# Six weight loads moved ahead of a branch and onto GpSimd's DMA queue, in a mixture-of-experts decoder layer

## The chip, the core and the metric

The kernel runs on one core of a Trainium2 chip. A core has five engines that follow their own instruction streams: TensorE (PE in the profile; its weight loads are PEld), VectorE (DVE), ScalarE (ACT), GpSimd (POOL) and SyncE (SP). SP does no arithmetic here; it issues transfers from the chip's main memory. Transfers issued by any engine are carried out by the core's 16 DMA engines. The metric is the device time of one execution in microseconds (us); smaller is better.

## What is computed

One layer of a hybrid decoder for 256 tokens of width 1024, all in 32-bit floats: two token mixers and an output projection, then a mixture of experts (MoE), then a gated embedding and a norm. The change lies in the MoE. Each token is given the two best of 32 experts, and each expert is a small gated network (the reference, cut; `xt` are the normed tokens, `wr` the routing weights):

```python
def blk(args):                       # one block of rows of one expert e
    ...
    xb = xt[toks]
    hid = jax.nn.silu(xb @ w_gate[e]) * (xb @ w_up[e])      # 1024 -> 512
    return ((hid @ w_down[e]) * wr[:, None]).astype(xt.dtype)  # 512 -> 1024
...
y = jax.ops.segment_sum(yb.reshape(n_pad, d), row_tok, num_segments=T)
```

No row may be dropped: an expert takes as many tokens as are sent to it.

## The kernel before

The mixers come first, then the experts in order, 0 to 31, in eight groups of four (`QUAD`, `NQ`, the loop over `q`). Each expert has room for 32 tokens (`CAP`). For a group, `dispatch` (L739) gathers the tokens of its four experts with one-hot matmuls (tile `px`, L761) into `xe`. For each expert, `expert` (L785) multiplies by the gate and up weights (`pg`, L810, eight blocks `k` of the 1024 inputs), applies SiLU (`sg`, L814) and the product (`hid`, L816), transposes (`pht`, L818, copied to `hT`), and multiplies by the down weights (`pd`, L827) into `eo`. After four experts `combine` (L837; tile `ps`, L839) adds the group's rows back into the tokens `h`.

An expert's weights are 6 MB: two loads of gate and up weights (here gu1 for blocks 0 to 3 and gu2 for blocks 4 to 7, 2 MB each, L712) and one load of down weights (dn, 2 MB, L717). I write 16gu1 for the first load of expert 16, 16dn for its last. Each load takes one slot of a ring of ten slots of 2 MB (`NRING`, all tiles named `wt`), in program order. A slot is written again when the matmuls on its old contents are done, so a load takes the slot of the load ten places before it: 16gu1 takes that of 12dn, 18gu1 that of 14dn, 18dn that of 15gu2, and 19gu2 that of 16gu1.

All loads are issued by SP, in order. Each of SP's loads signals one of eight completion semaphores in turn (`DMAHW0` to `DMAHW7` in the rows below), and waits until the load before it on the same semaphore has landed. So SP never has more than eight loads under way.

A token beyond the 32 of an expert is handled by `overflow` (L845), which stands after group 3 (`LOOP_AT`). It counts the rows per expert, works out how many extra blocks there are (`n_it`, L875), and every engine reads that number (L876) and branches on it:

```python
n_rv = nc.values_load(n_it[0:1, 0:1], min_val=0, max_val=NITEM, ...)   # L876
with tc.If(n_rv > 0):                                                  # L878
    with tc.For_i(0, n_rv, 1):                                         # L879
```

With these inputs the loop body is not entered. A scheduler orders the instructions of each engine between such branches; in the kernel before it has put the two gate and up loads of expert 16 ahead of the branch on SP, and all later ones behind it. On the way past the branch SP executes an instruction that waits for all eight of its completion semaphores.

Of the kernel before, what the change touches and what calls it, by code (L numbers as in the profile page):

```python
# [29 lines left out]
QUAD = 4  # L30
# [7 lines left out]
LO_POOL = (11, 101)  # L38
NRING = 10
LOOP_AT = 3  # L40

MIX = ["aq", "ak", "av", "mq", "mk", "mv", "mo", "ga", "ga1", "gm", "gm1"]
IN_OFF = dict(aq=0, ak=512, av=1024, mq=1536, mk=2048, mv=2560, mo=3072, mi=3584, mf=3588,
# [4 lines left out]
def layer(ctx: ExitStack, tc: tile.TileContext, A, dbg=None):  # L48
    nc = tc.nc
# [9 lines left out]
    def slot(shape, dt=F32, name="wt"):  # L59

        return ring.tile(shape, dt, name=name, tag="ring")
# [20 lines left out]
    for nm, src in (  # L82
# [7 lines left out]
        n = src.shape[0]  # L90
# [57 lines left out]
    for c in range(2):  # L148
        t = slot([P, 2, 4, 512])
# [66 lines left out]
    def split(dst_hi, dst_lo, src, scale=None, lo_on=None, low=False):  # L216

        if scale is None:
            a = nc.scalar.activation(dst_hi, src, AF.Copy)  # L219
            b = (lo_on or nc.vector).tensor_tensor(dst_lo, src, dst_hi.bitcast(F32), op=OP.subtract)  # L220
        else:
            a = nc.scalar.activation(dst_hi, src, AF.Copy, scale=scale)
            b = nc.vector.scalar_tensor_tensor(dst_lo, src, scale, dst_hi.bitcast(F32),
                                               op0=OP.mult, op1=OP.subtract)
        return b if low else a
# [63 lines left out]
    for k in range(KD):  # L289
# [13 lines left out]
        wt = wts["mq"][:, k].rearrange("p (f n) -> p f n", f=4)  # L303
# [280 lines left out]
    for f in range(0, KD, 2):  # L584
        pA = psf.tile([P, 2, T], F32, name="po", tag="po", bufs=3)
        wt, c0 = wup[f // 4], (f % 4) * P
# [121 lines left out]

    wgu_v, wd_v = A["expert_gu"], A["expert_down"]

    def load_gu(t, e, k0, n):
        nc.sync.dma_start(out=t, in_=wgu_v[e][:, k0:k0 + n])  # L712
        return [t[:, k] for k in range(n)]

    def load_expert(e):
        def load_dn(t, j, n):
            nc.sync.dma_start(out=t, in_=wd_v[e][:, j:j + n])  # L717
            return [t[:, i] for i in range(n)]

        gu = load_gu(slot([P, 4, 2, 512]), e, 0, 4)  # L720
        if e == NRING // 3:

            for k in range(4, 6):
                gu += load_gu(mo.tile([P, 1, 2, 512], F32, name="ov", tag="ov"), e, k, 1)
            t = slot([P, 4, D])
            gu += load_gu(t[:, 0:2].rearrange("p k (a n) -> p k a n", a=2), e, 6, 2)
            dn = load_dn(t[:, 2:4], 0, 2) + load_dn(slot([P, 2, D]), 2, 2)
        else:
            gu += load_gu(slot([P, 4, 2, 512]), e, 4, 4)
            t = slot([P, 4, D])  # L730
            if e == NE - 1:
                dn = load_dn(t[:, 0:2], 0, 2) + load_dn(t[:, 2:4], 2, 2)
            else:
                dn = load_dn(t, 0, 4)
        return gu, dn
# [101 lines left out]
    def combine(dwT, eo, n, b, c):  # L837
        ps = psm.tile([P, 512], F32, name="ps", tag="ps", bufs=2)
        mm(ps, dwT[0:n, b], eo[0:n, c * 512:(c + 1) * 512], start=True, stop=True)  # L839
        cs = slice(c * 512, (c + 1) * 512)  # L840
        return nc.vector.tensor_tensor(h[:, b, cs], ps, h[:, b, cs], op=OP.add)
# [63 lines left out]
    def embed():  # L905
        wpp = slot([P, 2, D], name="wpp")
        nc.sync.dma_start(out=wpp, in_=A["w_ple_proj"])
        ES = slot([P, 4096], name="ES")
        pin = ES[:, 0:512].rearrange("p (b n) -> p b n", b=NB)
        pT = ES[:, 512:1024].rearrange("p (k t) -> p k t", k=2)  # L910
        pe = ES[:, 1024:3072].rearrange("p (b n) -> p b n", b=NB)
        gfin = ES[:, 3072:4096]
        nc.sync.dma_start(out=pin, in_=A["p"].rearrange("l o (b p) d -> p (l o b) d", p=P))
        pp = psm.tile([P, 2, T], F32, name="pp", tag="tp", bufs=2)
        for k in range(2):
            for b in range(NB):
                nc.tensor.transpose(pp[:, k, b * P:(b + 1) * P], pin[:, b, k * P:(k + 1) * P], ident)
        nc.scalar.activation(pT, pp, AF.Copy)
        for b in range(NB):
            for c in range(2):  # L920
                ps = psm.tile([P, 512], F32, name="ps", tag="ps", bufs=2)
                for k in range(2):
                    mm(ps, pT[:, k, b * P:(b + 1) * P], wpp[:, k, c * 512:(c + 1) * 512],  # L923
                       start=(k == 0), stop=(k == 1))
                nc.scalar.activation(pe[:, b, c * 512:(c + 1) * 512], ps, AF.Copy, scale=0.5)
        return pe, gfin


    def load_gate():
        out = []  # L930
        for q in range(2):
            wt = slot([P, 4, D])
            for k in range(0, 4, 2):
                nc.sync.dma_start(out=wt[:, k:k + 2], in_=A["w_ple_gate"][q][:, k:k + 2])
            out.append(wt)
        nc.sync.dma_start(out=gfin, in_=A["final_norm_g"].rearrange("(o d) -> o d", o=1).to_broadcast([P, D]))
        return out

    def split_gate(k):
# [2 lines left out]
        hi, lo = gw[k // 4]  # L942
        return split(hi[:, k % 4], lo[:, k % 4], wpl[k // 4][:, k % 4], lo_on=nc.gpsimd if k in (0, 1, 3, 5) else None)

    for q in range(NQ):
        dwT, xe, rest = dispatch(float(q * QUAD * ESTR) if q else None, code, P)
        eo = mo.tile([P, D], F32, name="eo", bufs=1)
        for i in range(QUAD):
            e = q * QUAD + i
            wt = load_expert(e)  # L950
            if e == NE - 1:
                wpl = load_gate()
            expert(wt, xe, i, eo, 32 * i, last=(e == NE - 1), rest=rest if i == 0 else None)
        if q < NQ - 1:
            for c in range(2):
                for b in range(NB):
                    combine(dwT, eo, P, b, c)
        if q == LOOP_AT:
            overflow()
        if q == NQ - 3:  # L960
            pe, gfin = embed()
# [135 lines left out]
```

## Time and profile before

| | |
|---|---|
| time, median of 3 runs (lowest to highest) | 706.93 us (704.91 to 707.18) |
| the profiled execution: its time / its span | 706.04 us / 704.3 us |
| busy share of the span, PE / DVE / ACT / POOL | 80% / 40% / 26% / 5% |
| moved by DMA | 241.98 MB, mean 344 GB/s |
| chain that ended last: DMA / PE | 48% / 44% |

The span is what the trace covers; the 1.7 us between it and the execution's time lie outside. The chain is the sequence of work that ended last, followed back from the end; its DMA share is time in which an engine at the end of the chain waited for a transfer. Busy shares are averages over stages with different limits: the first 220 us or so are the mixers, with PE busy and DMA in part; from there to about 660 us run the experts.

### The profile page before, as it was taken

The numbers are of one execution on the slowest core, as the hardware profiler recorded it, in microseconds if no ns is written. First come the engines' busy times: TensorE is split into PE (matmuls) and PEld (weight loads), VectorE is DVE, ScalarE is ACT, GpSimd is POOL, SyncE is SP. The second block draws the span as 40 slices with busy tenths as digits, with TensorE's granted clock in tenths as the row PEclk, the third lists the DMA queues.
The fourth block names the chain that finished last, engine by engine and source line by source line (L and its number), as shares of the span: only waits on it lengthen the run. The fifth ranks groups of instructions, "written<-read, shape, count | busy, mean of one in ns | idle before, by whom it ended". The sixth has DMA issues, their size and how long they took to land.

```text
span 704.3 us, 12210 instructions
## 1 busy us (share of the span) xinstructions
PE 560.9 (80%) x5161; PEld 382.3 (54%) x5161; DVE 280.7 (40%) x684; ACT 186.1 (26%) x423; POOL 38.2 (5%) x59
## 2 busy tenths in 40 slices
PE   7999999999999998685686564967746956765894
PEld 7898778899986554342334231733423433432384
DVE  4898667676665343141022024312211310311175
ACT  6675556465453211001000000010000210000163
POOL 3000000001300000000000000000000000000063
PEclk9999999999999999899669886898978997988998
DMA  7946533338777899999999997999999999999921
GB/s 268 429 205 248 228 122 120 120 120 333 305 327 299 333 428 428 428 424 429 423 428 426 430 426 316 429 423 430 426 426 424 425 427 427 429 428 424 419 99 60
DMA packets 22130, 241.98 MB, mean 344 GB/s; under 512 B 4708, under 2 KB 5304, under 8 KB 7096
## 3 DMA queue, kind: packets, MB, share of 16 engines
q1 hardware_dynamic: 22056, 241.16, 82.5%
q8 instruction: 42, 0.69, 0.4%
q14 instruction: 16, 0.13, 0.0%
q10 hardware_dynamic: 16, 0.00, 0.0%
HBM read 240.10 MB, written 1.05 MB: 342 GB/s over the span
## 4 chain that ended last, share of the span: by engine, by line
DMA 48%; PE 44%; DVE 4%; ACT 2%; issue 1%; POOL 1%; POOLq 0%; SPq 0%; DVEq 0%; ACTq 0%
DMA wt<-in_expert_gu 31%; DMA wt<-in_expert_down 17%; PE pg L810 5%; PE po L330 4%; PE po L331 4%; PE po L332 4%; PE ps L839 3%; PE po L347 2%; PE po L346 2%; PE po L348 2%; PE pd L827 2%; PE px L761 2%; PE ps L923 1%; PE pyy L470 1%; DMA wt<-in_w_mix 1%
## 5 line engine op out<-in xcount | busy, mean ns | idle before, releaser
L810 PE MATMUL pg<-wt,xe 128*32 128x256 f32 x2032 | 153.6, 438 | 69.8 <-DMA wt<-in_expert_gu 69.8
L810 PEld LDWEIGHTS pg<-wt,xe 128*32 128x32 f32 x2032 | 73.3, 122 | 136.8 <-issue 55.6
L827 PE MATMUL pd<-wt,hT 128*32 128x256 f32 x1024 | 73.6, 434 | 22.8 <-DMA wt<-in_expert_down 18.6
L833 DVE COPY eo<-pd 32x256 f32<-32x256 f32 x64 | 27.1, 423 | 114.5 <-ACT eo L835 114.4
L827 PEld LDWEIGHTS pd<-wt,hT 128*32 128x32 f32 x1024 | 37.9, 121 | 47.4 <-issue 32.9
L835 ACT ACTIVATE eo<-pd 32x256 f32<-32x256 f32 x64 | 23.9, 374 | 150.3 <-PE pd L827 132.0
L816 DVE TENSOR_TENSOR hid<-sg,pg 128x128 f32<-128x128 f32 x32 | 9.2, 288 | 126.0 <-ACT sg L814 126.0
L220 DVE TENSOR_TENSOR wlo<-wt,whi 128x512 fp32r<-128x512 f32 x76 | 51.5, 685 | 18.3 <-ACT whi L219 18.1
L219 ACT ACTIVATE whi<-wt 128x512 fp32r<-128x512 f32 x77 | 47.3, 626 | 32.0 <-PE po L348 16.7
L814 ACT ACTIVATE sg<-pg 128x128 f32<-128x128 f32 x32 | 8.9, 277 | 168.7 <-PE pg L810 168.6
L761 PE MATMUL px<-og,y 128*128 128x128 f32 x256 | 39.6, 308 | 10.3 <-DVE og L752 6.8
L761 PEld LDWEIGHTS px<-og,y 128*128 128x128 f32 x256 | 35.5, 216 | 22.1 <-PEq L878 7.7
L839 PE MATMUL ps<-eo,dwT 128*128 128x512 f32 x64 | 34.2, 661 | 8.8 <-DVE eo L833 8.7
L332 PE MATMUL po<-XT,wlo 128*128 128x256 f32 x144 | 40.4, 280 | 1.0 <-DVE wlo L220 1.0
L330 PE MATMUL po<-XT,whi 128*128 128x256 f32 x144 | 40.6, 282 | 0.0
L331 PE MATMUL po<-XT,whi 128*128 128x256 f32 x144 | 40.3, 280 | 0.0
L765 DVE TENSOR_TENSOR xe<-px,cols 128x256 f32<-128x256 f32 x32 | 13.6, 424 | 61.5 <-PE pg L810 38.9
L220 POOL TENSOR_TENSOR glo<-wt,ghi 128x1024 fp32r<-128x1024 f32 x4 | 10.6, 2671 | 449.4 <-DMA wt<-in_w_ple_gate 448.6
L332 PEld LDWEIGHTS po<-XT,wlo 128*128 128x128 f32 x144 | 27.0, 188 | 1.2 <-DVE wlo L220 1.2
L220 DVE TENSOR_TENSOR spare<-wt,spare 128x512 fp32r<-128x512 f32 x34 | 23.3, 687 | 9.9 <-ACT spare L219 9.8
L331 PEld LDWEIGHTS po<-XT,whi 128*128 128x128 f32 x144 | 27.1, 188 | 0.2 <-issue 0.2
L330 PEld LDWEIGHTS po<-XT,whi 128*128 128x128 f32 x144 | 27.1, 188 | 0.0
(371 smaller groups left out, 956.9 us busy)
## 6 DMA issues: line engine op xcount, KB each, us to landing
wt<-in_expert_gu SPq DMA_DIRECT2D x63, 2048.0 KB, 38.2
wt<-in_expert_down SPq DMA_DIRECT2D x30, 2048.0 KB, 36.5
wt<-in_w_mix SPq DMA_DIRECT2D x10, 2048.0 KB, 22.2
wt<-in_w_up SPq DMA_DIRECT2D x2, 2048.0 KB, 8.5
wt<-in_w_out SPq DMA_DIRECT2D x2, 2048.0 KB
wt<-in_expert_down SPq DMA_DIRECT2D x4, 1024.0 KB
wt<-in_w_ple_gate SPq DMA_DIRECT2D x4, 1024.0 KB, 27.0
wt<-in_w_mix SPq DMA_DIRECT2D x4, 512.0 KB, 7.0
```

The lines of the kernel that those rows point to most:

```text
L219: a = nc.scalar.activation(dst_hi, src, AF.Copy)
L220: b = (lo_on or nc.vector).tensor_tensor(dst_lo, src, dst_hi.bitcast(F32), op=OP.subtract)
L330: mm(out[:, f], whi[:, kk], ahi[:, k], start=(k == 0), stop=False)
L331: mm(out[:, f], whi[:, kk], alo[:, k], start=False, stop=False)
L332: mm(out[:, f], wlo[:, kk], ahi[:, k], start=False, stop=(k == kn - 1))
L346: mm(outs[b], ahi[:, k, bs], whi[:, k - k0], start=(k == 0), stop=False)
L761: ins = mm(px[:, k], y[:, b, kc:kc + P], og[:, b], start=(b == 0), stop=(b == NB - 1))
L810: ins = pe(mm(pg[32 * j:32 * j + 32], xe[:, k, 32 * i:32 * i + 32], gu[k][:, :, j * P:(j + 1) * P], start=(k == 0), stop=(k == KD - 1)))
L827: pe(mm(pd[32 * c:32 * c + 32], hT[:, 32 * j:32 * j + 32], dn[j][:, c * 256:(c + 1) * 256], start=(j == 0), stop=(j == 3)))
L833: nc.vector.tensor_copy(out=dst, in_=pd[32 * c:32 * c + 32])
L835: nc.scalar.activation(dst, pd[32 * c:32 * c + 32], AF.Copy)
L839: mm(ps, dwT[0:n, b], eo[0:n, c * 512:(c + 1) * 512], start=True, stop=True)
```

## The change

Two experts (`NPOOL`), 16 and 17, have their loads issued ahead of the overflow branch, on GpSimd's queue. `load_expert` is called for them before `overflow()`, and the group loop takes the loaded tiles instead of loading again. All other loads stay on SP.

```diff
@@ -708,13 +709,17 @@
+    def queue(e):
+        return nc.gpsimd if QUAD * (LOOP_AT + 1) <= e < QUAD * (LOOP_AT + 1) + NPOOL else nc.sync
+
     def load_gu(t, e, k0, n):
-        nc.sync.dma_start(out=t, in_=wgu_v[e][:, k0:k0 + n])
+        queue(e).dma_start(out=t, in_=wgu_v[e][:, k0:k0 + n])
...
         def load_dn(t, j, n):
-            nc.sync.dma_start(out=t, in_=wd_v[e][:, j:j + n])
+            queue(e).dma_start(out=t, in_=wd_v[e][:, j:j + n])
@@ -942,12 +947,13 @@
+    ahead = {}
     for q in range(NQ):
...
-            wt = load_expert(e)
+            wt = ahead.pop(e, None) or load_expert(e)
...
         if q == LOOP_AT:
+            for e in range(QUAD * (q + 1), QUAD * (q + 1) + NPOOL):
+                ahead[e] = load_expert(e)
             overflow()
```

Three places of the program show what moves. First GpSimd's own stream around the branch. `n_it` is the number of extra blocks, `PE_49` stands for a wait on matmuls, `DMAHW…` for a wait on an earlier load by SP. Before:

```order
L638 TENSOR_TENSOR r_2271<-r_2271,mhalf 128x2 [waits DVE_49]
L876 TENSOR_LOAD n_it [waits DVE_49]
L878 COMPARE_AND_BRANCH
L879 COMPARE_AND_BRANCH
L879 UNCONDITIONAL_BRANCH
```

After (lines have moved by 1 to 5):

```order
L639 TENSOR_TENSOR r_2271<-r_2271,mhalf 128x2 [waits DVE_49]
L717 DMA wt<-in_expert_gu 128x4096 [waits DMAHW2_49,DMAHW3_49,DMAHW1_49,DMAHW7_49,PE_49,Activation_49]
L717 DMA wt<-in_expert_gu 128x4096 [waits DMAHW2_49,DMAHW4_49,DMAHW0_49,PE_49]
L722 DMA wt<-in_expert_down 128x4096 [waits DMAHW6_49,DMAHW5_49,PE_49]
L717 DMA wt<-in_expert_gu 128x4096 [waits DMAHW6_49,PE_49]
L717 DMA wt<-in_expert_gu 128x4096 [waits DMAHW7_49,PE_49]
L722 DMA wt<-in_expert_down 128x4096 [waits DMAHW0_49,PE_49]
L881 TENSOR_LOAD n_it [waits DVE_49]
L883 COMPARE_AND_BRANCH
```

The six loads of experts 16 and 17 stand between an operation of the mixers' end and the reading of `n_it`. Each waits only for its own slot: for the loads that filled it in earlier rounds, and for the matmuls on them.

Second, SP ahead of the branch; the first two rows are 15gu2 and 15dn. Before:

```order
L712 DMA wt<-in_expert_gu 128x4096 [waits DMAHW3_49,PE_49]
L717 DMA wt<-in_expert_down 128x4096 [waits DMAHW4_49,PE_49]
L712 DMA wt<-in_expert_gu 128x4096 [waits DMAHW5_49,PE_49]
L712 DMA wt<-in_expert_gu 128x4096 [waits DMAHW6_49,PE_49]
L876 TENSOR_LOAD n_it [waits DVE_49]
```

After:

```order
L717 DMA wt<-in_expert_gu 128x4096 [waits DMAHW3_49,PE_49]
L722 DMA wt<-in_expert_down 128x4096 [waits DMAHW4_49,PE_49]
L717 DMA wt<-in_expert_gu 128x4096 [waits DMAHW5_49,DMAHW1_49,PE_49]
L717 DMA wt<-in_expert_gu 128x4096 [waits DMAHW6_49,DMAHW2_49,PE_49]
L881 TENSOR_LOAD n_it [waits DVE_49]
```

Still two gate and up loads stand between 15dn and the branch, but they are now 18gu1 and 18gu2, and they take the slots of 14dn (`DMAHW1`) and 15gu1 (`DMAHW2`), where 16gu1 and 16gu2 took those of 12dn and 13gu1.

Third, SP on its way past the branch. Before, with 16dn, 17gu1, 17gu2, 17dn and so on:

```order
L878 UNCONDITIONAL_BRANCH [waits SP_sequencer_49,DMAHW0_49,DMAHW1_49,DMAHW2_49,DMAHW3_49,DMAHW4_49,DMAHW5_49,DMAHW6_49,DMAHW7_49]
L717 DMA wt<-in_expert_down 128x4096 [waits DMAHW7_49,PE_49]
L712 DMA wt<-in_expert_gu 128x4096 [waits DMAHW0_49,PE_49]
L712 DMA wt<-in_expert_gu 128x4096 [waits DMAHW1_49,PE_49]
L717 DMA wt<-in_expert_down 128x4096 [waits DMAHW2_49,PE_49]
```

After, with 18dn, 19gu1, 19gu2, 19dn, 20gu1:

```order
L883 UNCONDITIONAL_BRANCH [waits SP_sequencer_49,DMAHW0_49,DMAHW1_49,DMAHW2_49,DMAHW3_49,DMAHW4_49,DMAHW5_49,DMAHW6_49,DMAHW7_49]
L722 DMA wt<-in_expert_down 128x4096 [waits DMAHW7_49,DMAHW3_49,PE_49]
L717 DMA wt<-in_expert_gu 128x4096 [waits DMAHW4_49,DMAHW0_49,PE_49]
L717 DMA wt<-in_expert_gu 128x4096 [waits DMAHW1_49,DMASW0_49,PE_49]
L722 DMA wt<-in_expert_down 128x4096 [waits DMAHW2_49,DMASW1_49,PE_49]
L717 DMA wt<-in_expert_gu 128x4096 [waits DMAHW3_49,DMASW2_49,PE_49]
```

The wait for SP's own eight semaphores is still there, and the six of GpSimd's loads (`DMASW0` to `DMASW5`) are not among them. The first load behind it is now 18dn; from the third on (19gu2) a load takes a slot that GpSimd filled, so it waits for a matmul of expert 16 or 17.

## Rows read from the trace of the kernel before

**Rows 1.** The page: slices of 17.6 us; DMA in tenths, GB/s moved.
```profile
DMA  7946533338777899999999997999999999999921
GB/s 268 429 205 248 228 122 120 120 120 333 305 327 299 333 428 428 428 424 429 423 428 426 430 426 316 429 423 430 426 426 424 425 427 427 429 428 424 419 99 60
```

**Rows 2.** The page: shares of the last chain; then queues (packets, MB, share).
```profile
DMA 48%; PE 44%; DVE 4%; ACT 2%; issue 1%; POOL 1%; POOLq 0%; SPq 0%; DVEq 0%; ACTq 0%
...
q1 hardware_dynamic: 22056, 241.16, 82.5%
q8 instruction: 42, 0.69, 0.4%
q14 instruction: 16, 0.13, 0.0%
q10 hardware_dynamic: 16, 0.00, 0.0%
```

**Rows 3.** SP's loads in time: start, duration, count; a pair's span includes waiting.
```profile
381.27 0.33 SPq L717 DMA_DIRECT2D wt<-in_expert_down  x1
386.15 5.23 SPq L712 DMA_DIRECT2D wt<-in_expert_gu  x2
430.34 0.34 SPq L717 DMA_DIRECT2D wt<-in_expert_down  x1
430.78 0.85 SPq L712 DMA_DIRECT2D wt<-in_expert_gu  x2
...
434.46 14.86 SPq L712 DMA_DIRECT2D wt<-in_expert_gu  x2
451.13 0.33 SPq L717 DMA_DIRECT2D wt<-in_expert_down  x1
454.68 0.33 SPq L712 DMA_DIRECT2D wt<-in_expert_gu  x1
```

**Rows 4.** PE's matmuls in time; in brackets the idle time before, and its end.
```profile
378.04 1.93 PE L827 MATMUL pd<-wt,hT 128*32 128x256 f32 x32 [0.39 <-DVE hT L821]
381.35 1.93 PE L810 MATMUL pg<-wt,xe 128*32 128x256 f32 x32 [1.37 <-DMA wt<-in_expert_gu]
386.14 1.93 PE L810 MATMUL pg<-wt,xe 128*32 128x256 f32 x32 [2.86 <-DMA wt<-in_expert_gu]
...
410.72 2.92 PE L810 MATMUL pg<-wt,xe 128*32 128x256 f32 x32 [2.96 <-DMA wt<-in_expert_gu]
415.51 3.30 PE L810 MATMUL pg<-wt,xe 128*32 128x256 f32 x32 [1.88 <-DMA wt<-in_expert_gu]
...
439.58 6.70 PE L761 MATMUL px<-og,y 128*128 128x128 f32 x32 [6.81 <-DVE og L752]
446.21 1.48 PE L810 MATMUL pg<-wt,xe 128*32 128x256 f32 x18
...
447.88 1.06 PE L810 MATMUL pg<-wt,xe 128*32 128x256 f32 x14
...
454.42 3.66 PE L810 MATMUL pg<-wt,xe 128*32 128x256 f32 x64
...
461.28 1.94 PE L810 MATMUL pg<-wt,xe 128*32 128x256 f32 x32
```

**Rows 5.** What SP waited for, 360 to 470 us: total us, times, longest.
```profile
SPq L876 <- DVE n_it L875: 31.6, 1, 31.6
...
SPq L878 <- SPq L878: 6.2, 3, 4.9
```

**Rows 6.** Windows: stretch, us, busy time by engine, PE's clock, DMA share, GB/s.
```profile
350.00:400.00 50.00, 34.79 (x357) 17.53 (x357) 10.46 (x26) 3.83 (x11) 0.00 (x0) 0.83 1.01 427
...
425.00:434.00 9.00, 6.55 (x8) 2.42 (x8) 4.44 (x12) 0.37 (x1) 0.00 (x0) 0.62 0.58 209
...
431.00:434.00 3.00, 1.77 (x3) 0.41 (x2) 1.60 (x4) 0.00 (x0) 0.00 (x0) 0.83 0.92 284
...
450.00:500.00 50.00, 38.81 (x458) 22.38 (x450) 12.61 (x35) 4.48 (x13) 0.00 (x0) 0.90 1.01 427
```

More of the change, by code (lines that the diff above doesn't have):

```diff
@@ L40 @@
 LOOP_AT = 3
+NPOOL = 2
 MIX = ["aq", "ak", "av", "mq", "mk", "mv", "mo", "ga", "ga1", "gm", "gm1"]
```

## The prediction

> **What bounds the kernel now.** I read the slices first: from slice 14 on the DMA row is 9 nearly without a break, at 424 to 430 GB/s, and the one low slice among them, 316 GB/s, is the one with the branch (slice 24, 422 to 440 us) [rows 1]. Then the chain of work that ended last: 48% of it is DMA, 44% PE [rows 2]. Then PE's matmuls in time: the matmuls on 13gu1 and 13gu2 start at 381.35 and 386.14 after waiting for a load, and SP issues its next loads at 381.27 and 386.15, the same instants [rows 3, 4]. So the expert part runs at the pace of the loads, PE waits for each, and each landing lets SP issue the load eight places later. At 427 GB/s [rows 6] a load of 2,097,152 bytes takes 4.9 us, an expert 14.7 us. Where PE does not wait it needs less: expert 16's down matmuls give way to expert 17's at 454.42 and those to 18's at 461.28, 6.9 us apart [rows 4]. What counts is therefore whether the DMA engines ever stand still before the end; a late PE costs nothing as long as they do not. PE gains some 7.8 us per expert on the loads, less what group changes cost it.
>
> **What the branch costs now.** SP issues 16gu2 at about 391.4 (386.15 plus 5.23) and then waits 31.6 us, to 423.0, for `n_it` [rows 3, 5]. Its next load goes out at 430.34. In between stands the instruction that waits for all eight of SP's semaphores, that is until 16gu2 has landed: 15gu2 landed by 415.5 [rows 4], then come 15dn, 16gu1 and 16gu2 at 4.9 us each, so 430.2. That agrees with 430.34, and with a wait of SP on itself at the branch of up to 4.9 us [rows 5]. So DMA runs dry and has to start again. From 425 to 434 us it moved 209 GB/s instead of 427 [rows 6]: 9.0 x (1 - 209/427) = 4.6 us of transfer lost. That is all there is to gain. Behind the wait SP has eight loads' worth of free slots and issues 16dn to 19gu1 from 430.34 to about 434.9 [rows 3]; that is 39 us of work. The ninth, 19gu2, has to wait for the slot of 16gu1, which PE leaves at 448.94 (447.88 plus 1.06) [rows 4], and SP issues it at about 449.0 (434.46 plus 14.86, less its own 0.33) [rows 3]. By then DMA is still busy, to about 431.3 + 39.2 = 470.5.
>
> **Change, part 1: where the six loads go.** GpSimd has nothing to do in this stretch (POOL is busy 0.00 us in each window shown [rows 6]) and its loads wait for their slots alone, so 16gu1 goes out when PE leaves 12dn, at 380.0 (378.04 plus 1.93 [rows 4]), not at 386.15. SP at that time has eight loads under way, 13gu1 to 15gu2, and adds 15dn at 381.27. The DMA engines now have two queues, and what matters is how they share. The trace shows practically one queue: SP's moves 241.16 of 241.98 MB, GpSimd's has no row, and the others are instruction fetches and one 4 KB load [rows 2]. So the share is not measured. Its bounds are nothing for GpSimd until SP's queue is empty, and everything for GpSimd whenever it has a load. I take equal shares, since all these loads are the same size and shape.
>
> The Trainium skill ("DMA: Bandwidth & Descriptors", section on queues, rings and completion order) says that a DMA engine goes round the queues that have work, one packet each. If packets are alike, that gives equal shares and the sum below; no run here shows it.
>
> With equal shares each load takes 9.8 us. GpSimd's next load can go only when a load of SP's has landed and PE has used it (16gu2 after 13gu1, 16dn after 13gu2, 17gu1 after 13dn, 17gu2 after 14gu1, 17dn after 14gu2). So the two queues step one for one. The six loads of GpSimd take 59 us, in which SP's six loads 13gu2 to 15gu1 land at half pace. With more than an equal share for GpSimd the order is the same, as its next load still waits for one of SP's. After that SP's queue is alone: 15gu2, 15dn, 18gu1 (issued when PE leaves 14dn) and 18gu2 (when PE leaves 15gu1). PE reaches 15gu2 six loads later than now, 6 x 4.9 = 29 us, at about 445. No transfer time is lost up to here, only the order differs.
>
> **Part 2: the wait at the branch.** `n_it` comes 7.5 us after 15gu2 (423.0 less 415.5), and 18gu2 lands three loads, 14.7 us, after it, exactly as 16gu2 did. GpSimd's loads have all landed by then, about 19 us earlier. So SP drains its queue with nothing else moving, and the 4.6 us are lost as before. Change: 0.
>
> **Part 3: behind the branch.** All times here are in the old timeline, 29 us to be added. SP resumes at 430.34 and can issue 18dn and 19gu1 (slots of 15gu2 and 15dn). The third, 19gu2, needs the slot of 16gu1, and PE gets to that only after the branch, the dispatch (`px` from 439.58) and its own first matmuls: 448.94, as now. Nothing shortens that path, since 16gu1 had landed before it in the old kernel too. Two loads are 9.8 us of work: from 431.3 (issue plus about 1 us until bytes move; from 431 on they do [rows 6]) to 441.1. The next bytes move at 449.0 plus 1 = 450.0. DMA stands still for 8.9 us. It then starts up a second time: from 431 to 434 it moved 284 instead of 427 GB/s, 3.0 x (1 - 284/427) = 1.0 us lost, of which 0.3 are counted already, so 0.7 more. Bounds: 8.9 without that, 9.9 with all of the 1.0. I take 9.5.
>
> **Part 4: afterwards.** PE has 16gu1 to 19gu1, ten loads, in hand and frees slots about every 2.5 us, DMA fills one in 4.9 us, so it does not stop again. PE is 29 us late but gains on the loads: with 58.8 us of loads per group against some 28 to 33 us of experts and 12 to 15 us of combine and dispatch (`px` start to `pg` is 6.6 us [rows 4], the combine about as much), 11 to 19 us per group. Four groups remain, so 44 us at least; it is back on the loads' heels before expert 31, and the end is set by the last load, as now. GpSimd's issuing and the moved lines of the other engines cost nothing, as none of them ends the chain.
>
> **Sum.** 0 (drain) + 8.9 + 0.7 = 9.5 us of DMA standing still, at the end of a chain that DMA sets. The profiled execution took 706.04, of which 1.7 us lie outside the span of 704.3: 706.04 + 9.5 = 715.5. Its median is 706.93, 0.9 higher; with that 716.4. I say 716.0. A difference under 0.3%, 2.1 us, can't be told from none here.
>
> **Rivals.**
> First, **GpSimd's queue gets clearly less than SP's**, and the change becomes a gain. The place is the drain. If GpSimd's share is under about 0.55 of SP's, some of 16gu1 to 17dn are still moving when SP's queue runs dry at the branch, so DMA never stops, and they also fill the 8.9 us behind it. Followed load by load with the rules and durations above, at shares of 0.4 and 0.5 both holes close, and the whole 4.6 us come back, 701.5 to 702.5. At a quarter or less the experts 16 and 17 come in so late that PE has not freed slots for SP, and a new hole of 1.3 to 3.4 us opens: 703 to 708. Between 0.55 and 0.75 it is 708 to 714. For it: a GpSimd queue could cut rows into smaller packets. Against it: SP's queue moves its 241.16 MB in 22,056 packets, 10.9 KB on average with the small loads among them [rows 2], so rows of 16 KB go whole there, and nothing in the change cuts them differently. Chance 0.20, about half of it under 0.3% better than before or dearer.
> The skill's same page (section on SWDGE, HWDGE and iDMA) says that GpSimd's packets are preferably no longer than 4096 B. By that rule a quarter of SP's packet gives a quarter of its share, and the time would be the 703 to 708 of this rival. No trace here shows a packet of GpSimd's.
>
> Second, **two queues together move less than one**. Twelve loads, 59 us, move side by side. A tenth less costs 5.9 us more: 716 + 5.9 = 722. Nothing in the trace shows it, since only one queue carries weights; the nearest row is the full rate of that one. Chance 0.10.
>
> Third, **the change does not do what it says**: GpSimd's loads go out late, or the branch does not wait for SP's queue, and its 7.4 us between `n_it` and 430.34 are the branch itself. The first is excluded by the idle GpSimd. In the second the times at which SP resumes are the same, and so is the hole behind it; only a very early resume would shorten the drain, not the wait for 16gu1's slot: 711 to 716. It is within the forecast.
>
> **Chances.** Forecast 0.70 with 713 to 719 of its own; queue with a small share 0.20; slower together 0.10. The range 706 to 722 holds the forecast, the second rival and about a third of the first. Faster by over 0.3%: 0.13. Within 0.3%: 0.10. Slower by over 0.3%: 0.77.
>
> **What would show it.** In the new profile: six loads on GpSimd's queue from about 380; PE's waits in experts 13 and 14 doubled, with matmuls on successive loads some 9.8 us apart instead of 4.9; the matmuls on 15gu2 near 445; SP's next load near 460, two loads at once and the third 18 us later; a stretch of 0 GB/s near 471 to 479; then no waits of PE for loads through experts 16 to 18. It is wrong if the loads of experts 13 to 15 keep their 4.9 us pace (then the first rival), or if GB/s falls below 420 while both queues work (then the second).

## The result and the profile after

| | before | after |
|---|---|---|
| median of the runs (lowest to highest) | 706.57 us (704.91 to 707.18), 4 runs | 712.39 us (711.60 to 713.56), 4 runs |
| the profiled execution: time / span | 706.04 / 704.3 us | 713.56 / 711.8 us |

The changed kernel takes 1.0087 times as long (95% interval 1.0063 to 1.0112): 5.8 us more by the medians, where 9.5 were forecast. In the changed kernel lines have moved by up to 8: L717 and L722 issue the loads of experts, L815 is the matmul `pg`, L832 `pd`, L766 `px`, L883 the branch.

The page's slices, here of 17.8 us, with the DMA share in tenths and the GB/s, and then GpSimd's queue (packets, MB, share); they answer to [rows 1, 2]:

```profile
DMA  7947533339867999999999999769999999999921
GB/s 269 431 193 267 205 119 119 119 119 352 320 283 296 372 427 429 426 428 426 426 426 428 426 430 426 320 254 429 428 426 422 429 426 426 427 426 426 421 113 60
...
q0 software_dynamic: 864, 12.58, 4.2%
```

Where one slice was low, two are now: 320 and 254 GB/s. GpSimd's queue (q0) exists now and carries six loads, 12.58 MB. The loads of SP and of GpSimd in time (start, duration, count; a pair's duration includes the wait between the two; for GpSimd the idle time before, and what ended it):

```profile
428.94 10.34 SPq L717 DMA_DIRECT2D wt<-in_expert_gu  x2
460.57 0.34 SPq L722 DMA_DIRECT2D wt<-in_expert_down  x1
461.02 16.82 SPq L717 DMA_DIRECT2D wt<-in_expert_gu  x2
...
383.13 0.78 POOL L717 DMA_DIRECT2D wt<-in_expert_gu  x1 [162.28 <-ACT eo L840]
384.55 0.53 POOL L717 DMA_DIRECT2D wt<-in_expert_gu  x1 [0.63 <-PE pg L815]
390.51 0.53 POOL L722 DMA_DIRECT2D wt<-in_expert_down  x1 [5.43 <-PE pg L815]
400.19 0.53 POOL L717 DMA_DIRECT2D wt<-in_expert_gu  x1 [9.15 <-PE pd L832]
409.98 0.53 POOL L717 DMA_DIRECT2D wt<-in_expert_gu  x1 [9.27 <-PE pg L815]
419.69 0.53 POOL L722 DMA_DIRECT2D wt<-in_expert_down  x1 [9.18 <-PE pg L815]
```

From the third on, GpSimd's loads go out one by one, each when PE has left a slot, 9.7 to 9.8 us apart. SP's first load behind the branch goes out at 460.57, its second at 461.02, and its third at 477.51 (461.02 + 16.82 - 0.33), 16.5 us later. In the kernel before, eight went out at once [rows 3].

PE's matmuls on successive loads (in brackets the idle time before, and its end), to set beside [rows 4]:

```profile
396.23 3.64 PE L832 MATMUL pd<-wt,hT 128*32 128x256 f32 x32 [5.00 <-DMA wt<-in_expert_down]
406.02 3.64 PE L815 MATMUL pg<-wt,xe 128*32 128x256 f32 x32 [6.15 <-DMA wt<-in_expert_gu]
415.72 3.64 PE L815 MATMUL pg<-wt,xe 128*32 128x256 f32 x32 [6.06 <-DMA wt<-in_expert_gu]
...
445.10 3.64 PE L815 MATMUL pg<-wt,xe 128*32 128x256 f32 x32 [6.20 <-DMA wt<-in_expert_gu]
...
469.38 5.42 PE L766 MATMUL px<-og,y 128*128 128x128 f32 x32 [7.90 <-DVE og L757]
```

13dn, 14gu1 and 14gu2 arrive 9.8 and 9.7 us apart instead of 4.9; 15gu2 is reached at 445.10 instead of 415.51. What DMA did meanwhile: the windows (stretch, us, busy time by engine, PE's clock, DMA share, GB/s).

```profile
384.00:440.00 56.00, 21.96 (x198) 9.43 (x194) 3.08 (x9) 2.05 (x6) 2.64 (x5) 0.60 1.01 428
455.00:465.00 10.00, 5.35 (x8) 1.85 (x8) 4.38 (x11) 0.37 (x1) 0.00 (x0) 0.83 0.61 227
465.00:470.00 5.00, 0.61 (x3) 0.65 (x4) 1.51 (x6) 0.00 (x0) 0.00 (x0) 0.59 1.01 429
470.00:480.00 10.00, 10.00 (x106) 7.34 (x106) 4.22 (x16) 0.66 (x2) 0.00 (x0) 0.86 0.38 129
480.00:500.00 20.00, 19.19 (x299) 11.70 (x294) 5.23 (x15) 3.08 (x9) 0.00 (x0) 1.00 1.01 426
```

And the queues from 384 to 440 us (packets, MB, share):

```profile
q1 hardware_dynamic: 859, 12.50, 52.5%
q0 software_dynamic: 778, 11.44, 48.0%
```

While both queues work, they move 428 GB/s together and share them nearly evenly, 12.50 to 11.44 MB. Then there are two holes. Against 427 GB/s, the first costs 10 x (1 - 227/427) = 4.7 us, the second 10 x (1 - 129/427) = 7.0 us; between them DMA runs at full rate for 5 us on the two loads that SP could issue. Before, the one hole cost 4.6 us [rows 6]. The difference is 7.1 us; the spans differ by 7.5.

### The profile page after: what moved, and what is told of

Same layout as the page of the kernel before. It is cut to its first block, busy times and chain, and to the rows that moved or that the text cites. A ratio compares the mean times of both kernels' runs of the same rounds, so it can differ in the third digit from the quotient of the medians.

```text
span 711.8 us, 12217 instructions
## 1 busy us (share of the span) xinstructions
PE 558.5 (78%) x5161; PEld 380.6 (53%) x5161; DVE 282.0 (40%) x684; ACT 186.6 (26%) x423; POOL 41.0 (6%) x65
## 3 DMA queue, kind: packets, MB, share of 16 engines
q0 software_dynamic: 864, 12.58, 4.2%
## 5 line engine op out<-in xcount | busy, mean ns | idle before, releaser
L815 PE MATMUL pg<-wt,xe 128*32 128x256 f32 x2032 | 152.7, 435 | 77.0 <-DMA wt<-in_expert_gu 76.8
L815 PEld LDWEIGHTS pg<-wt,xe 128*32 128x32 f32 x2032 | 72.6, 122 | 140.8 <-DMA wt<-in_expert_gu 56.3
L832 PE MATMUL pd<-wt,hT 128*32 128x256 f32 x1024 | 74.6, 440 | 25.9 <-DMA wt<-in_expert_down 21.8
L832 PEld LDWEIGHTS pd<-wt,hT 128*32 128x32 f32 x1024 | 37.8, 124 | 52.6 <-issue 38.5
L766 PE MATMUL px<-og,y 128*128 128x128 f32 x256 | 37.9, 299 | 10.9 <-DVE og L757 7.9
L766 PEld LDWEIGHTS px<-og,y 128*128 128x128 f32 x256 | 33.8, 207 | 22.4 <-PEq L883 8.7
L846 DVE TENSOR_TENSOR h<-ps,h 128x512 f32<-128x512 f32 x32 | 22.1, 691 | 10.7 <-PE ps L844 10.7
```

Of the source, the lines that this page charges most:

```text
L766: ins = mm(px[:, k], y[:, b, kc:kc + P], og[:, b], start=(b == 0), stop=(b == NB - 1))
L815: ins = pe(mm(pg[32 * j:32 * j + 32], xe[:, k, 32 * i:32 * i + 32], gu[k][:, :, j * P:(j + 1) * P], start=(k == 0), stop=(k == KD - 1)))
L832: pe(mm(pd[32 * c:32 * c + 32], hT[:, 32 * j:32 * j + 32], dn[j][:, c * 256:(c + 1) * 256], start=(j == 0), stop=(j == 3)))
```

## The experiments

My theory after this: with two queues that share evenly, the loads of experts 16 and 17 overtake those of 13 to 15 and fill the ring, and behind SP's wait at the branch there is too little left to issue. The rivals: the second queue costs something per load; the move ahead of the branch costs it; the stop at the branch is the branch itself and not SP's wait for its loads. All diffs are against the changed kernel; each run is compared with runs of the kernel before on the same chip (706.56 us for one expert, three experts, the move without the queue and the queue behind the branch; 706.72 for the other three).

**One expert on GpSimd's queue.**

```diff
-NPOOL = 2
+NPOOL = 1
```

> One expert instead of two on GpSimd's queue (16 only, ahead of the branch). Theory (the cost is the ring: SP has too few free slots behind the branch): PE is delayed by three loads, 14.7 us, at the branch, SP drains as before, but behind the wait it has five loads to issue (17dn to 19gu1), 24.5 us of work, more than the 18.6 us until PE leaves 16gu1. No hole, so 706.5 us, ratio 0.997 to 1.003. Rival (two queues side by side, or software descriptors, cost time per load): half of the 5.8 us, 709.5 us, ratio 1.004.

Measured: 706.59 us, ratio 0.9998 (0.9989 to 1.0007). SP's loads behind the branch in time:

```profile
446.08 0.34 SPq L722 DMA_DIRECT2D wt<-in_expert_down  x1
446.53 0.84 SPq L717 DMA_DIRECT2D wt<-in_expert_gu  x2
447.47 0.84 SPq L722 DMA_DIRECT2D wt<-in_expert_down  x1
448.41 14.88 SPq L717 DMA_DIRECT2D wt<-in_expert_gu  x2
```

The windows around it:

```profile
400.00:440.00 40.00, 20.10 (x200) 9.00 (x196) 6.76 (x23) 2.42 (x7) 0.00 (x0) 0.60 1.01 428
440.00:450.00 10.00, 5.40 (x8) 1.95 (x8) 4.95 (x12) 0.37 (x1) 0.00 (x0) 0.83 0.59 225
450.00:500.00 50.00, 43.06 (x516) 28.73 (x520) 18.35 (x56) 4.87 (x14) 0.00 (x0) 0.93 1.01 426
```

Five loads go out at the branch, the sixth waits for 16gu1's slot until 462.96, and DMA has not run dry by then: one hole of 4.7 us, as in the kernel before, and no second. Three loads on the second queue cost nothing that shows (the interval ends 0.8 us below and 0.5 us above the kernel before), so there is no price per load of the size that the rival needs.

**Three experts on GpSimd's queue.**

```diff
-NPOOL = 2
+NPOOL = 3
```

> Three experts on GpSimd's queue ahead of the branch. Theory: the nine loads take all slots, SP has 19gu1 alone to issue around the branch, and 19gu2 waits for PE to leave 16gu1. DMA stands still for some 20 us in all instead of 4.6 before: 722 to 727 us, ratio 1.022 to 1.029. Rival (a cost per load on the second queue): one and a half times the 5.8 us, 715.3 us, ratio 1.012.

Measured: 716.29 us, ratio 1.0131 (1.0114 to 1.0147), less than the theory's 722 to 727 and next to the rival's 715.3. The windows tell which of the two it is:

```profile
440.00:460.00 20.00, 7.85 (x78) 3.47 (x72) 5.58 (x20) 0.28 (x1) 1.05 (x2) 0.67 1.01 427
460.00:470.00 10.00, 5.69 (x27) 1.81 (x18) 3.86 (x8) 0.74 (x2) 0.00 (x0) 0.84 0.74 296
470.00:480.00 10.00, 8.29 (x65) 6.74 (x65) 5.13 (x19) 0.00 (x0) 0.00 (x0) 0.71 0.01 2
480.00:485.00 5.00, 5.00 (x79) 2.82 (x80) 1.19 (x4) 0.66 (x2) 0.00 (x0) 1.00 0.81 292
```

Full rate until 460, then a standstill of ten us. Against 427 GB/s these rows lose 3.1 + 10.0 + 1.6 = 14.6 us, 10.0 more than before, and 9.7 were measured. So the place is the one that the theory names, and a cost per load would have shown as a lower rate while the queues work. What I had wrong was the length: I had taken PE's path from the last loads to 16gu1 as in the kernel before. PE starts on 15dn at 458.11 and leaves 16gu1 at 480.10, 22.0 us, against 28.5 before (420.49 to 448.94). PE's matmuls on that path, first the combine (`ps`) of the kernel before, then `ps` and `px` here, with the idle time before each in brackets:

```profile
426.22 6.55 PE L839 MATMUL ps<-eo,dwT 128*128 128x512 f32 x8 [3.80 <-DVE eo L833]
...
462.68 3.96 PE L844 MATMUL ps<-eo,dwT 128*128 128x512 f32 x8 [0.94 <-DVE eo L838]
471.71 5.72 PE L766 MATMUL px<-og,y 128*128 128x128 f32 x32 [5.07 <-DVE og L757]
```

Of the 6.5 us, 2.9 are the wait of the combine: in the kernel before, VectorE turns to `eo` only after its work on `n_it` and the blocks, at 425.74, whereas here 15dn lands so late that this work is done by then. Another 2.6 us are the combine itself (6.55 and 3.96 us; PE's granted clock was 0.62 in 425 to 434 us before [rows 6], and is 0.84 in 460 to 470 here), 1.7 the way from the combine past the branch to `px` (6.81 [rows 4] and 5.07), and 1.0 `px` (6.70 and 5.72); against them the matmuls on 15dn take 1.7 us longer (1.93 and 3.64).

**The move without the queue.**

```diff
-        return nc.gpsimd if QUAD * (LOOP_AT + 1) <= e < QUAD * (LOOP_AT + 1) + NPOOL else nc.sync
+        return nc.sync
```

> The move without the queue: the six loads of experts 16 and 17 ahead of the branch, but issued by SP in order. Theory (the second queue lets late loads overtake early ones and fill the ring): nothing overtakes; SP reads n_it at 423, drains what it has, the last of it 17dn at about 450, then has eight slots. DMA loses 4.6 us at the drain, as before: 706.5 us, ratio 0.997 to 1.003. Rival (it is the move ahead of the branch that costs): 712 us, ratio 1.008.

Measured: 706.30 us, ratio 0.9995 (0.9986 to 1.0004). SP's loads around the branch in time:

```profile
411.61 0.33 SPq L722 DMA_DIRECT2D wt<-in_expert_down  x1
451.17 0.82 SPq L717 DMA_DIRECT2D wt<-in_expert_gu  x2
```

What SP waited for at the branch (total us, times, longest):

```profile
SPq L883 <- SPq L883: 27.6, 4, 17.3
```

The windows:

```profile
400.00:445.00 45.00, 27.11 (x238) 15.68 (x237) 15.88 (x51) 2.05 (x6) 0.00 (x0) 0.80 1.00 426
445.00:455.00 10.00, 8.60 (x136) 4.80 (x130) 2.44 (x9) 1.69 (x5) 0.00 (x0) 1.00 0.62 236
```

The move alone neither gains nor costs: SP stands at the branch until the six loads behind 15dn, 16gu1 to 17dn, have landed (`n_it` is there at 422.6, when PE has already begun on 15dn, at 421.47; the next load goes out at 451.17), and DMA loses 4.5 us there. So the hole moves with the last load that SP issued before, and it is the wait for the loads that makes it.

**Nothing for SP to wait for.**

```diff
         if q == LOOP_AT:
-            for e in range(QUAD * (q + 1), QUAD * (q + 1) + NPOOL):
-                ahead[e] = load_expert(e)
             overflow()
```

The queue stays as it is: the scheduler puts 16 ahead of the branch, and leaves 17 and all of SP's loads from 18gu1 on behind it.

> The change without its loop ahead of the branch: experts 16 and 17 on GpSimd's queue, 16 ahead of the branch, 17 behind it, and nothing of SP's between 15dn and the branch. So SP has nothing to drain, and what is left is the branch itself. Theory: n_it still comes 7.5 us after 15gu2, the branch takes SP and GpSimd about 5 us more, and no load is moving from 15dn's landing on: DMA stands still for about 8.5 us and starts up, 9.2 us lost against 4.6 before: 711 us, ratio 1.005 to 1.008. Rival (the wait for SP's semaphores is all of the stop): SP passes as soon as n_it is there, the stop is 3 us, 704 to 706 us.

Measured: 709.63 us, ratio 1.0047 (1.0031 to 1.0062), between the two expectations. The first loads of GpSimd and of SP behind the branch:

```profile
438.13 1.04 POOL L717 DMA_DIRECT2D wt<-in_expert_gu  x2 [45.26 <-DVE it_e L870]
438.61 0.81 SPq L717 DMA_DIRECT2D wt<-in_expert_gu  x2
```

SP's wait there:

```profile
SPq L883 <- SPq L883: 0.5, 1, 0.5
```

The windows:

```profile
430.00:435.00 5.00, 2.31 (x35) 1.20 (x35) 1.32 (x7) 0.28 (x1) 0.00 (x0) 1.00 0.48 200
435.00:438.00 3.00, 2.29 (x31) 1.47 (x32) 2.79 (x9) 0.00 (x0) 0.00 (x0) 0.75 0.00 0
438.00:445.00 7.00, 5.56 (x16) 1.95 (x8) 4.14 (x11) 0.75 (x2) 1.56 (x3) 0.62 0.83 322
```

`n_it` is ready at 436.82; GpSimd's next load starts 1.3 us and SP's 1.8 us later. That is the price of the branch itself; I had put it at 5. DMA still stands longer than before, 2.7 + 3.0 + 1.7 = 7.4 us, because no load is under way between the landing of 15dn and `n_it`. The loads that SP waits for are at the same time the cover for the wait on `n_it`.

**The queue behind the branch.** If the hole is SP's wait, loads by an engine that has no such wait should fill it.

```diff
-        return nc.gpsimd if QUAD * (LOOP_AT + 1) <= e < QUAD * (LOOP_AT + 1) + NPOOL else nc.sync
+        return nc.gpsimd if e in (17, 18) else nc.sync
...
-            for e in range(QUAD * (q + 1), QUAD * (q + 1) + NPOOL):
-                ahead[e] = load_expert(e)
```

> The queue without the move: experts 17 and 18 on GpSimd's queue, issued behind the branch; 16gu1 and 16gu2 stay on SP ahead of it. Theory: GpSimd's way past the branch has no wait for SP's semaphores, so it issues its six loads at about 424 to 429, while 16gu2 is still moving; DMA does not run dry and most of the 4.6 us come back: 702 to 704 us, ratio 0.993 to 0.997. If GpSimd passes the branch late (as PE, which takes 5.8 us), the gain is half of it. Rival (any load on GpSimd's queue costs): 709 to 712 us, ratio 1.004 to 1.008.

Measured: 703.64 us, ratio 0.9961 (0.9947 to 0.9975). Part of the hole is filled. GpSimd's first load behind the branch:

```profile
428.32 1.32 POOL L717 DMA_DIRECT2D wt<-in_expert_gu  x2 [207.81 <-DMA wt<-in_expert_gu]
```

The windows:

```profile
425.00:430.00 5.00, 3.94 (x8) 1.33 (x8) 3.39 (x8) 0.58 (x2) 1.67 (x3) 0.97 0.73 279
430.00:435.00 5.00, 0.00 (x0) 0.00 (x0) 0.77 (x3) 0.00 (x0) 1.73 (x4) 0.72 0.91 367
```

What is left is 1.7 + 0.7 = 2.4 us. GpSimd's loads start at 428.32, 5.7 us after `n_it`, and the profile names a load as what ended the wait. It is not the branch that held GpSimd: its branch instruction starts at 423.6, 1.0 us after `n_it`. Which load it waited for, and why it waited longer here than the 1.3 us seen elsewhere, stays open.

**More cover.** Two variants keep more under way at the branch: expert 16 ahead of it on SP, 17 and 18 on GpSimd; and 16 and 17 ahead on SP, 18 and 19 on GpSimd.

```diff
-        return nc.gpsimd if QUAD * (LOOP_AT + 1) <= e < QUAD * (LOOP_AT + 1) + NPOOL else nc.sync
+        return nc.gpsimd if e in (17, 18) else nc.sync
...
-            for e in range(QUAD * (q + 1), QUAD * (q + 1) + NPOOL):
+            for e in (16,):
                 ahead[e] = load_expert(e)
```

> Meant to close the hole: the three loads of expert 16 ahead of the branch on SP, experts 17 and 18 on GpSimd's queue (17gu1 and 17gu2 come out ahead of the branch, 17dn and 18 behind it). Theory: when SP drains, three loads of its own and then four of GpSimd's are moving, and GpSimd passes the branch some 5 us after n_it without waiting for SP; GB/s stays above 400 through the branch, SP then has 19gu1 and soon freed slots. The whole 4.6 us come back: 701.5 to 703 us, ratio 0.993 to 0.995. Rival (the gain of e4 came from something else than cover): no better than e4, 703.6 us or more.

Measured: 703.00 us, ratio 0.9950 (0.9936 to 0.9963). The hole is gone; GpSimd's loads behind the branch go out 21 us before SP's next, as the loads in time show:

```profile
433.31 0.53 POOL L722 DMA_DIRECT2D wt<-in_expert_down  x1 [32.33 <-SPq L883]
...
454.18 1.51 SPq L717 DMA_DIRECT2D wt<-in_expert_gu  x2
```

The window of the branch:

```profile
425.00:455.00 30.00, 18.43 (x140) 11.61 (x140) 14.54 (x47) 1.02 (x3) 2.08 (x4) 0.83 1.01 426
```

This is faster than both kernels. By its time it can't be told from the queue behind the branch (703.64 us, on another chip): the intervals of the two ratios overlap, so what the added cover gave is seen in the hole alone.

```diff
-        return nc.gpsimd if QUAD * (LOOP_AT + 1) <= e < QUAD * (LOOP_AT + 1) + NPOOL else nc.sync
+        return nc.gpsimd if e in (18, 19) else nc.sync
...
-            for e in range(QUAD * (q + 1), QUAD * (q + 1) + NPOOL):
+            for e in (16, 17):
                 ahead[e] = load_expert(e)
```

> The same with more cover: experts 16 and 17 ahead of the branch on SP, in order, experts 18 and 19 on GpSimd's queue (18gu1 and 18gu2 ahead of the branch, 18dn and 19 behind it). Theory: SP's own queue is full through the branch, and when it drains near 470, GpSimd's last two loads still move. 701.5 to 703.5 us, ratio 0.993 to 0.996. If GpSimd's loads are through before SP's queue, the 4.6 us are lost again later: 706.5 us.

Measured: 706.51 us, ratio 0.9998 (0.9989 to 1.0007). The first expectation fell, and the second one, loads of GpSimd's through before SP's queue, is what came. The rate holds through the branch and breaks later, in the windows:

```profile
440.00:475.00 35.00, 18.53 (x184) 11.65 (x187) 7.16 (x25) 1.41 (x4) 1.06 (x2) 0.74 1.01 426
475.00:485.00 10.00, 9.37 (x132) 5.15 (x124) 1.98 (x6) 1.30 (x4) 0.00 (x0) 0.87 0.63 246
```

The two queues run dry at about the same time, SP's next load goes out at 479.43, and 4.2 us are lost at 475 to 485 instead.

One sum holds for all of them. The transfer time lost in the holes around the branch, from the windows against 427 GB/s, less the 4.6 us of the kernel before, beside the difference of the medians:

| kernel | lost in holes, us | less 4.6 | measured, us |
|---|---|---|---|
| the change | 4.7 + 7.0 | +7.1 | +5.8 |
| one expert | 4.7 | +0.1 | 0.0 |
| three experts | 14.6 | +10.0 | +9.7 |
| move on SP | 4.5 | -0.1 | -0.3 |
| nothing to wait for | 7.4 | +2.8 | +2.9 |
| queue behind | 2.4 | -2.2 | -2.9 |
| cover with 16; 17, 18 | 0.0 | -4.6 | -3.7 |
| cover with 16, 17; 18, 19 | 4.2 | -0.4 | -0.2 |

The holes are read from one execution of each kernel, the times are medians of several. By the spans of those same executions the sum holds within 0.9 us in seven kernels and misses in one: the cover with 16 and 17, 18 has a span of 702.0 us, 2.3 less than before, where 4.6 were to be gained. Why is not shown.

## Why the prediction was right, and where it was off

**The bound** was right: the end follows the DMA engines' standstills, by the medians within 1.3 us in eight kernels, and PE's 29 us of delay at the branch cost nothing by themselves. Near the end of the changed kernel PE waits for loads again.

**Part 1, equal shares**, the open term, came out at 12.50 to 11.44 MB. The rate of both together was 428 GB/s. With that the first two rivals fall: GpSimd's share was 0.92 of SP's, and the two queues did not move less than one. The time alone would not have told: the first rival's 708 to 714 at shares of 0.55 to 0.75 holds it too. Its packets are no smaller: 12.58 MB in 864 packets are 14.6 KB on average. The Trainium skill says that a DMA engine goes round its queues packet by packet ("DMA: Bandwidth & Descriptors", section on queues, rings and completion order); the equal shares agree with that. The Trainium skill's preference for packets of at most 4096 B ("DMA: Bandwidth & Descriptors", section on SWDGE, HWDGE and iDMA) is not what these rows of 16 KB came to, as the profile counts packets.

**Part 2, the drain unchanged**, was right: 4.7 against 4.6 us, at 460.57, where "near 460" was said. That it is a wait for loads, and not the branch, which the third rival had left open, is shown by two runs: 27.6 us of waiting with six loads to land, 0.5 us with none.

**Part 3, two loads and then nothing**, was right in its mechanism: third load 16.5 us after the second, DMA at 16 GB/s or less from 473 to 478. The size was off: 9.5 forecast (its terms add up to 9.6), 7.0 measured. The main part is the sentence "nothing shortens that path". 16gu1's slot came free some 1.7 us earlier (477.51 against 449.00 plus the 30.2 by which SP's first load behind the branch moved, 479.23). Of these, 1.3 are the gather `px`, which took 6.70 us before [rows 4] and 5.42 after; 0.4 had been gained before `px` began. PE's granted clock is the last figure but two in the windows, first of the kernel before, then of the changed one:

```profile
440.00:445.00 5.00, 5.00 (x25) 5.00 (x25) 1.06 (x3) 0.00 (x0) 0.00 (x0) 0.50 1.01 426
...
470.00:475.00 5.00, 5.00 (x39) 4.79 (x42) 1.45 (x5) 0.00 (x0) 0.00 (x0) 0.72 0.43 180
```

So the shorter `px` goes with a higher clock: 0.50 before, the lower level of 1.2 GHz throughout, and 0.72 after, partly the upper level of 2.4 GHz. In both PE had stood idle ahead of `px`, for 6.8 and 7.9 us, and I have no run that tells why the levels differ. Of the rest, 0.8 us, some 0.7 I had counted twice: the start after the drain is in the 4.6 us already, and the two loads that follow it last longer by what it costs, so the hole behind them is shorter.

**Part 4** was right: no further hole, 426 GB/s from 480 to 500 us, and PE through experts 16 to 19 with hardly a wait.

The effect lies in the direction of the forecast, at about two thirds of its size. The time, 712.39, lies in the range of 706 to 722, but just below the 713 to 719 that the prediction gave its own mechanism. Of the 3.7 us between 9.5 and 5.8, 2.5 are the size of the hole; the rest is less than the 1.7 us by which the profiled executions, from which the hole is read, lie further apart (7.5 us) than the medians (5.8).

## What to carry to other kernels

Where transfers set the pace, a load issued earlier on a second queue adds no bandwidth (428 GB/s with two queues here, 427 with one); it takes its share from the loads that are needed first, and holds a buffer from then until it is used. Count, at the point where the issuing engine resumes, how many buffers are free, and how long until the next comes free: if their loads take less time than that, a hole is left. A second queue pays at a place where the first must wait for all its loads, if it is still moving something there (2.9 and 3.7 us gained here); so have loads of it to issue at the wait, and not all of them long ahead of it.

## What the runs showed that I had not expected

The branch on a value in memory costs the issuing engines 1.3 us (GpSimd) to 1.8 us (SP) from the value to the next load, in the run where SP has nothing to wait for; the rest of the 7.4 us between `n_it` and SP's next load in the kernel before was the wait for loads. GpSimd spends 0.53 us on a load of 2 MB, 0.78 on the first, so its own work is no limit here. And two queues with equally large loads share the DMA engines to within a tenth (12.50 to 11.44 MB), with the same total as one (428 and 427 GB/s).
